# Expert slots dealt to the partitions in another order, and row gathers and stores over 128 partitions

## The chip, the core and the metric

The program runs on one core of one Trainium2 chip. A core has five engines that run their own instruction lists and meet only at semaphores: TensorE (PE, with its weight loads shown apart as PEld), VectorE (DVE), ScalarE (ACT), GpSimd (POOL) and SyncE (SP). Transfers are issued from SP's and from POOL's list and are carried by 16 DMA engines. The metric is the device time of one execution in microseconds (us), and the median of the runs is what counts.

## The reference

One decoder layer on 2048 tokens of width 1024, all in float32:

```python
h = rmsnorm(x, norm1_w)
x = x + mixer(h, w_in, ret_gn_w, conv_w, w_o)      # retention and short convolution
h = rmsnorm(x, norm2_w)
g_sel = top_1(softmax(h @ router_g_w + router_g_b))            # one group of 8
top_p, top_i = top_2(softmax(h @ router_e_w[g_sel] + ...))     # two of its 8 experts
y = segment_sum(gate * (silu(xb @ w_gate[e]) * (xb @ w_up[e])) @ w_down[e])
out = rmsnorm(x + y, final_norm_w)
```

There are 64 experts, each with 6 MB of weights (two matrices of 1024 by 512 and one of 512 by 1024). Each token goes to two experts, so the 64 experts receive 4096 rows in all, 64 on average.

## The kernel before

The first part (up to about 930 us in the profile) computes the mixer, adds the residual, writes the sums to the output in DRAM and the normalised rows to a DRAM tensor `h_rows`, and routes the tokens. Each token gets, for each of its two experts, a rank: how many earlier tokens chose that expert. `record` writes token number, a flag and the gate to a list in DRAM at slot `rank * 64 + expert` (indirect stores over 128 partitions, 128 indices each). Before the last 512 tokens are known, `load_list` reads the list of ranks 0 to 95 into the tile `listed`, rank r in partition r; the last 512 tokens are put in by TensorE (`place`), with a 0/1 matrix `here` that says which partition a rank belongs to. The sum is the tile `ix` of token numbers, one column for each expert, one partition for each of the 96 slots (`CAP`). A slot that holds no token has a number far above 2047.

The second part runs over 64 experts in a fixed order (`order`: one expert of each group in turn). The weights of an expert come as six transfers of 1024 KB ("units"), 128 partitions by 8 KB, issued from SP as soon as one of the buffers is free (14 buffers in the steady state, a little over two experts' worth). Most units are split by ACT (`split_hi`, L671) and DVE (`split_lo`, L677) into a rounded part and a remainder, and TensorE multiplies three products for each (L727 to L729); a quarter is multiplied whole (L1043).

The rows of an expert make three trips through POOL's queue, each one an indirect DMA with a column of `ix` as its indices: `gather` fetches normalised rows from `h_rows` (issued three experts ahead, L698), TensorE transposes them (`xpose`, L718), `regather` fetches the same tokens' residual rows from the output into the same tile (L705), the expert's result is added by DVE (`add_rows`), and `put_rows` stores them to the output (L811). Indices above 2047 are out of bounds and move nothing. A row is 4096 bytes. Seven row tiles are in use in turn. With these three trips an expert moves 3 x 4096 bytes for each of its rows.

On ACT, DVE and PE the order of work is the order in which the code is written. A transposed row tile is copied out of PSUM by ACT (L721) and DVE (L722), in the same two instruction lists that split the units.

Of the kernel before, what the change touches and what calls it, by code (L numbers as in the profile page):

```python
# [10 lines left out]
F32 = mybir.dt.float32  # L11
F32R = mybir.dt.float32r
BF16 = mybir.dt.bfloat16
I32 = mybir.dt.int32
U32 = mybir.dt.uint32
AF = mybir.ActivationFunctionType
OP = mybir.AluOpType
AX = mybir.AxisListType

P = 128  # L20
S = 2048
D = 1024
KD = D // P
# [4 lines left out]
NE = 64  # L28
# [3 lines left out]
CAP = 96  # L32
RANKS = CAP + S
NONE = 1 << 20
EPS = 1e-6
NROW = 7
# [8 lines left out]
Q, K, V, G, F0, F1, F2, O0, O1 = range(9)  # L45
CONV = {F0: "ccuu", F1: "ccuu", F2: "bbbb"}
CN = dict(ident=(0, 128), mhalf=(128, 132), tok=(148, 164), slots=(164, 260),
          mask=(260, 388), tri=(388, 516), vdec=(516, 520), odec=(520, 524), cdec=(524, 528))
NCON, NKEEP = 528, 260


def host_constants():
    f = np.float32
    c = np.zeros((P, NCON), f)
    i = np.arange(P)

    def put(name, a):
        lo, hi = CN[name]
        c[:, lo:hi] = a

    put("ident", np.eye(P))
    put("mask", i[:, None] <= i[None, :])
    put("tri", i[:, None] < i[None, :])
    log_g = np.log1p(-(2.0 ** (-5.0 - np.arange(H)))).astype(f).astype(np.float64)
    put("vdec", np.exp(-log_g[None] * (i[:, None] + 1)))
    put("odec", np.exp(log_g[None] * (i[:, None] + 1)) * P ** -0.5)
    put("cdec", np.exp(log_g * P)[None])
    put("tok", np.arange(S // P)[None] * P + i[:, None] - NONE)
    put("mhalf", -0.5)
    put("slots", np.arange(96)[None])  # L70
    inv = (10000.0 ** (-np.arange(64) / 64)).astype(f)
    ang = (np.arange(S).astype(f)[:, None] * inv[None]).astype(np.float64)
    cos, sin = np.cos(ang).T.astype(f), np.sin(ang).T.astype(f)
    rot = np.stack([np.concatenate([cos, cos]), np.concatenate([sin, -sin])], 1)
    empty = np.zeros((RANKS * NE, 4), f)
    return c, np.ascontiguousarray(rot), empty
# [3 lines left out]
def hybrid_layer(ctx: ExitStack, tc: tile.TileContext, x, xT, norm1, w_in, gn_w, conv_w, w_o, norm2, norm2r,  # L80
                 r_w, r_b, w_gate, w_up, w_down, final_w, con, rot, empty, out):
    nc = tc.nc
    act, dve, pool, pe, sp = nc.scalar, nc.vector, nc.gpsimd, nc.tensor, nc.sync

    h_d = nc.dram_tensor("h_rows", (S, D), F32, kind="Internal").ap()
    list_d = nc.dram_tensor("slots", (RANKS * NE, 4), F32, kind="Internal").ap()
# [6 lines left out]
    base = ctx.enter_context(tc.tile_pool(name="base", bufs=1, side="left"))  # L93
# [10 lines left out]
    def cst(name):  # L104
        lo, hi = CN[name]
        return cons[:, lo:hi] if hi <= NKEEP else cons2[:, lo - NKEEP:hi - NKEEP]

    ident, mask = cst("ident"), cst("mask")
# [84 lines left out]
    tri = late.tile([P, P], BF16, name="tri")  # L193
# [77 lines left out]
    rt = {}  # L271
# [228 lines left out]
    def small(shape, name, dt=F32, bufs=1, pool=late):  # L500
        return pool.tile([P] + shape, dt, name=name, bufs=bufs)

    def bc(ap, shape):
        return ap.to_broadcast([P] + shape)

    iota = cst("slots")
# [28 lines left out]
    def gates(b, i):  # L535
        c = rt["c", i]
        z, rec = c["z"], c["rec"]
        dve.reciprocal(z[:, 3:5], z[:, 3:5])
        dve.tensor_scalar(z[:, 0:3], z[:, 0:3], z[:, 3:4], None, op0=OP.mult)
        dve.reciprocal(z[:, 2:3], z[:, 2:3])  # L540
        dve.tensor_scalar(rec[:, :, 3], z[:, 0:2], z[:, 4:5], z[:, 2:3], op0=OP.mult, op1=OP.mult)
# [7 lines left out]
    def rank2(b, i):  # L549
        c = rt["c", i]  # L550
        prod = small([2, NE], "prod")
        rk, key = (small([2], n, bufs=2) for n in ("rk", "key"))
        dve.tensor_tensor(prod, c["full"], bc(c["p"][:, None, :NE], [2, NE]), op=OP.mult)
        dve.tensor_reduce(rk, prod, axis=AX.X, op=OP.add)
        if b == NB - 1:
            c["here"] = small([2, CAP], "here", bufs=2)
            dve.tensor_tensor(c["here"], bc(iota[:, None, :CAP], [2, CAP]), bc(rk[:, :, None], [2, CAP]), op=OP.is_equal)
        dve.scalar_tensor_tensor(key, rk, float(CAP), c["e64"], op0=OP.is_ge, op1=OP.add)
        for j in range(2):
            dve.tensor_tensor(c["rec"][:, j, 2:3], key[:, j:j + 1], key[:, 1 - j:2 - j], op=OP.is_gt)  # L560
        c["rk"], c["slot"] = rk, small([2], "slot", I32, bufs=8, pool=base)
# [18 lines left out]

    def load_list():
        t = late.tile([CAP, NE, 4], F32, name="listed")
        sp.dma_start(t, list_d[:CAP * NE].rearrange("(s e) r -> s e r", e=NE))
        pool.tensor_scalar(t[:, :, 0], t[:, :, 0], float(NONE), None, op0=OP.add)
        rt["listed"] = t

# [31 lines left out]
    EX = {}  # L618
# [55 lines left out]
    def split_lo(i):  # L674
        if i < len(pieces):
            hi, lo, src = parts[pieces[i]]
            dve.tensor_tensor(lo, src, hi.bitcast(F32), op=OP.subtract)  # L677
# [3 lines left out]
    def moved(kind, q, ins):  # L681
        for (k2, q2), o in rows_dma.items():
            if order[q2] // 8 != order[q] // 8:
                tc.declare_no_dep(ins.ins, o.ins, reason="tokens of another group")
        rows_dma[kind, q] = ins

    def row_of(q):
        return EX["rows"][q % NROW]

    def spaced(t=spacer):  # L690
        pool.memset(t, 0.0)

    def gather(q):
        if q >= NE:
            return
        e = order[q]
        spaced()
        pool.indirect_dma_start(out=row_of(q), out_offset=None, in_=h_d,  # L698
                                in_offset=bass.IndirectOffsetOnAxis(ap=EX["ix"][:, e:e + 1], axis=0),
                                bounds_check=S - 1, oob_is_err=False)  # L700

    def regather(q):
        e = order[q]
        spaced()
        i = pool.indirect_dma_start(out=row_of(q), out_offset=None, in_=out,  # L705
                                    in_offset=bass.IndirectOffsetOnAxis(ap=EX["ix"][:, e:e + 1], axis=0),
                                    bounds_check=S - 1, oob_is_err=False)
        moved("g", q, i)
# [100 lines left out]
    def put_rows(q):  # L809
        spaced()  # L810
        i = pool.indirect_dma_start(out=out, out_offset=bass.IndirectOffsetOnAxis(ap=EX["ix"][:, order[q]:order[q] + 1], axis=0),  # L811
                                    in_=row_of(q), in_offset=None, bounds_check=S - 1, oob_is_err=False)
        moved("s", q, i)


# [11 lines left out]
    for b in range(NB):  # L827
# [12 lines left out]
        for g in (F0, F1):  # L840
            for j in range(2):
                f = j + 2 * (g == F1)
# [16 lines left out]
        if b < NB - 1:  # L859
# [5 lines left out]
            for i in range(TB):  # L865
# [7 lines left out]
                at(so + 2 * i + 7, address, b, i)  # L873
                at(so + 2 * i + 7, record, b, i)
    at(start[NB - 1, F1], load_list)

    for k in range(KD):
# [24 lines left out]
    b = NB - 1  # L902
# [46 lines left out]
    i = TB - 1  # L949
# [9 lines left out]
    rank1(b, i)  # L959
    spread(i, dve, 0)  # L960
    rank2(b, i)
    place(i, 0)
    gates(b, i - 1)
    ix = base.tile([CAP, NE], I32, name="ix")
    li, sec, nsec = (base.tile([CAP, NE], F32, name=n) for n in ("li", "sec", "nsec"))
    EX.update(li=li, ix=ix, sec=sec, nsec=nsec)
    listed = rt["listed"]
    dve.tensor_tensor(ix, listed[:, :, 0], rt["pslot", 0][:CAP, :NE], op=OP.add)
    split_lo(0)
    split_lo(1)  # L970
    spread(i - 1, dve, 2)
# [9 lines left out]

    w = ctx.enter_context(tc.tile_pool(name="work", bufs=1, side="right", reuse_waits="tile"))
    EX["work"] = w
    EX["rows"] = [w.tile([CAP, D], F32, name=f"row{i}") for i in range(3)]

    def clear(q):
        act.activation(row_of(q).rearrange("p (a b) -> p a b", b=P),
                       ident[:CAP, None, :].to_broadcast([CAP, KD, P]), AF.Copy, scale=0.0)

    def pair(tag):  # L990
        t = raw.tile([P, 2, D], F32, name="pair", tag=tag)
        return [t[:CAP, i] for i in range(2)]

    for q in range(3):
        clear(q)
# [2 lines left out]
    for q in range(3):  # L998
        gather(q)
    split_lo(2)  # L1000
    xpose(0)
    regather(0)
    for k in range(3, LEAD):
        split_lo(k)
# [9 lines left out]
    for i, (q, wi, c) in enumerate(estream):  # L1014
# [7 lines left out]
        if i in (36, 40, 44):  # L1022
            two = pair(FIRST[i // 4 - 9])
            if i < 44:
                EX["rows"] += two
                for j in (2, 1):
                    clear(len(EX["rows"]) - j)
                    if i == 36:
                        gather(5 - j)
            else:  # L1030
                EX["fw"], EX["fwm"] = two
                sp.dma_start(EX["fw"], bass.AP(tensor=final_w.tensor, offset=final_w.offset, ap=[[0, CAP], [1, D]]))
        n = q, 2 * wi + c // 4
        cs = slice(c % 4 * 512, c % 4 * 512 + 512)
# [12 lines left out]
        if wi < 2:  # L1047
# [3 lines left out]
            if wi == 0 and c == 0:  # L1051
                if q > 1:
                    gather(q + 3)
                if later(q - 2):
                    weights(q - 2)
            if wi == 0 and c == 2 and 1 < q < NG + 2:
                put_rows(q - 2)
# [12 lines left out]
        else:  # L1070
# [15 lines left out]
            else:  # L1086
                if c == 1:
                    norm1_rows(q - 1)
                if c == 2:
                    r = row_of(q - 1)  # L1090
# [114 lines left out]
```

## Time and profile before

| | |
|---|---|
| runs | 2198.74, 2205.43, 2206.37 us, median 2205.43 |
| profiled execution | 2198.08 us, of which the span of instructions is 2196.3 us |
| granted TensorE clock, mean | 0.988 of full speed |
| PE busy | 2127.2 us, 97% of the span |
| DVE, ACT, POOL busy | 73%, 56%, 40% |
| moved by DMA | 578.70 MB, mean 263 GB/s |
| of that from SP's queue and from POOL's queue | 526.43 MB and 50.44 MB |

"Share" of DMA is the mean busy share of the 16 DMA engines; it can come out a little over 1, since a packet's time is taken from its start to its end and neighbours overlap slightly. A matmul's busy time overlaps the next one's, so PE at 97% says less than the pace at which experts follow one another, for which the issue of each expert's `regather` is a good mark: it stands once in each expert, behind the transposition of that expert's rows.

### The profile page before, as it was taken

How to read it: one execution, taken by the hardware profiler on the slowest of the kernel's cores; microseconds unless marked ns; L12 is line 12 of the kernel's file. 1: busy time of each engine (PE TensorE's matmuls, PEld its weight loads, DVE VectorE, ACT ScalarE, POOL GpSimd, SP SyncE). 2: the span in 40 equal slices, each digit the busy share in tenths (PEclk: the TensorE clock that was granted, in tenths of full speed). 3: DMA queues.
4: the chain of work that ended last, by engine and by line, in shares of the span. 5: the costliest groups of instructions: out<-in, count | busy, mean ns of one | idle time of the engine just before them, and what ended most of it. 6: DMA issues, size and time to landing. Idle time of an engine off the chain costs nothing. (4 is left out here: it accounts for less than half of the span.)

```text
span 2196.3 us, 28309 instructions
## 1 busy us (share of the span) xinstructions
PE 2127.2 (97%) x9673; PEld 1562.2 (71%) x9674; DVE 1612.1 (73%) x2393; ACT 1226.1 (56%) x1881; POOL 871.1 (40%) x927
## 2 busy tenths in 40 slices
PE   8999999999999999789999999999999999999997
PEld 7888888888888888666666666666666665666664
DVE  5667566656666666678888888878888787788886
ACT  5324342433343323566667777767676666667674
POOL 0020031002200120341247777666555655565657
PEclk9999999999999999899999999999999999999999
DMA  8335344524443456689999999999999999999994
GB/s 269 117 99 179 96 144 130 168 87 154 128 160 96 135 156 237 231 285 352 365 368 369 367 360 353 356 355 362 357 359 350 356 352 353 355 355 352 358 356 158
DMA packets 136100, 578.70 MB, mean 263 GB/s; under 512 B 23440, under 2 KB 23792, under 8 KB 86736
## 3 DMA queue, kind: packets, MB, share of 16 engines
q1 hardware_dynamic: 113424, 526.43, 67.9%
q0 software_dynamic: 22528, 50.44, 7.1%
q8 instruction: 76, 1.25, 0.2%
q14 instruction: 72, 0.59, 0.1%
HBM read 559.94 MB, written 44.20 MB: 275 GB/s over the span
## 5 line engine op out<-in xcount | busy, mean ns | idle before, releaser
L677 DVE TENSOR_TENSOR ring<-unit,ring 128x1024 fp32r<-128x1024 f32 x428 | 557.9, 1325 | 124.4 <-ACT ring L671 122.7
L671 ACT ACTIVATE ring<-unit 128x1024 fp32r<-128x1024 f32 x428 | 444.4, 1054 | 232.5 <-DMA unit<-in_w_gate_dram 105.5
L291 PE MATMUL acc<-hhi,ring 128*128 128x512 f32 x1280 | 403.8, 393 | 6.9 <-ACT ring L166 5.8
L677 DVE TENSOR_TENSOR part<-unit,part 128x1024 fp32r<-128x1024 f32 x212 | 275.8, 1314 | 57.7 <-ACT part L671 57.0
L167 DVE TENSOR_TENSOR ring<-wraw,ring 128x512 fp32r<-128x512 f32 x256 | 172.7, 687 | 185.1 <-ACT ring L166 184.9
L166 ACT ACTIVATE ring<-wraw 128x512 fp32r<-128x512 f32 x256 | 154.0, 626 | 263.9 <-issue 111.0
L727 PE MATMUL acc<-ring,xhi 128*96 128x512 f32 x684 | 288.4, 422 | 4.4 <-ACT xhi L721 4.0
L729 PE MATMUL acc<-ring,xlo 128*96 128x512 f32 x684 | 272.9, 399 | 16.0 <-DVE xlo L722 16.0
L671 ACT ACTIVATE part<-unit 128x1024 fp32r<-128x1024 f32 x212 | 221.0, 1054 | 115.7 <-DMA unit<-in_w_gate_dram 42.9
L291 PEld LDWEIGHTS acc<-hhi,ring 128*128 128x128 f32 x1280 | 241.0, 188 | 56.3 <-ACT ring L166 5.5
L728 PE MATMUL acc<-ring,xhi 128*96 128x512 f32 x684 | 272.5, 398 | 0.0
L291 PE MATMUL acc<-hlo,ring 128*128 128x512 f32 x640 | 249.9, 390 | 0.0
L1043 PE MATMUL acc<-unit,ewhole 128*96 128x512 f32 x512 | 230.3, 592 | 0.0
L291 PE MATMUL acc<-ring,mix 128*128 128x512 f32 x768 | 185.4, 396 | 0.0
L729 PEld LDWEIGHTS acc<-ring,xlo 128*96 128x96 f32 x684 | 111.9, 164 | 71.9 <-DVE xlo L722 24.2
L291 PEld LDWEIGHTS acc<-ring,mix 128*128 128x128 f32 x768 | 142.7, 189 | 28.5
L291 PE MATMUL acc<-ring,hhi 128*128 128x512 f32 x512 | 162.3, 398 | 0.0
L1043 PEld LDWEIGHTS acc<-unit,ewhole 128*96 128x96 f32 x512 | 83.5, 163 | 110.6 <-issue 101.5
L727 PEld LDWEIGHTS acc<-ring,xhi 128*96 128x96 f32 x684 | 113.6, 166 | 63.4 <-ACT xhi L721 14.5
L728 PEld LDWEIGHTS acc<-ring,xhi 128*96 128x96 f32 x684 | 112.3, 164 | 50.3 <-issue 6.6
L727 PE MATMUL acc<-part,xhi 128*96 128x512 f32 x340 | 143.4, 422 | 4.7 <-ACT xhi L721 4.7
L783 POOL TENSOR_TENSOR pair<-pair 96x1024 f32<-96x1024 f32 x31 | 84.5, 2726 | 152.2 <-ACT pair L780 152.1
(229 smaller groups left out, 3732.5 us busy)
## 6 DMA issues: line engine op xcount, KB each, us to landing
unit<-in_w_down_dram SPq DMA_DIRECT2D x128, 1024.0 KB, 25.2
unit<-in_w_gate_dram SPq DMA_DIRECT2D x128, 1024.0 KB, 25.5
unit<-in_w_up_dram SPq DMA_DIRECT2D x128, 1024.0 KB, 26.8
wraw<-in_w_in_dram SPq DMA_DIRECT2D x225, 256.0 KB, 2.9
wraw<-in_w_o_dram SPq DMA_DIRECT2D x64, 256.0 KB, 2.9
xs<-in_x_dram SPq DMA_DIRECT2D x16, 512.0 KB, 4.8
x<-in_x_dram SPq DMA_DIRECT2D x16, 512.0 KB, 4.0
out_dram<-x SPq DMA_DIRECT2D x16, 512.0 KB, 4.0
```

Of the source, the lines that this page charges most:

```text
L166: act.activation(hi, src, AF.Copy)
L167: dve.tensor_tensor(lo, src, hi.bitcast(F32), op=OP.subtract)
L291: pe.matmul(o, l, r, start=first and j == 0, stop=last and j == 2)
L671: act.activation(t[:, 0], src, AF.Copy)
L677: dve.tensor_tensor(lo, src, hi.bitcast(F32), op=OP.subtract)
L727: pe.matmul(o, ahi, whi, start=first, stop=False)
L728: pe.matmul(o, ahi, wlo, start=False, stop=False)
L729: pe.matmul(o, alo, whi, start=False, stop=last)
L783: pool.tensor_tensor(r, r, m, op=OP.mult)
L1043: pe.matmul(o, whole[:, k - hi.shape[1]], wt, start=False, stop=last)
```

## The change

The ranks are dealt to the partitions in another order, by the table `RUNS`: partitions 0 to 31 hold ranks 0 to 31, partitions 32 to 63 hold ranks 64 to 95, partitions 64 to 95 hold ranks 32 to 63. The list is loaded by three transfers of 32 partitions instead of one of 96, and `here` compares with a row of constants `ranks` (96 columns more in the constants) instead of the plain count 0 to 95. The tile of indices grows to 128 partitions; the upper 32 are set out of bounds by one DVE instruction. The row tiles are 128 partitions high, and gathers, regathers and stores name all 128 partitions; the arithmetic still works on the first 96.

```diff
+RUNS = (0, 64, 32)
+    put("ranks", np.concatenate([np.arange(r, r + 32) for r in RUNS])[None])
...
-            dve.tensor_tensor(c["here"], bc(iota[:, None, :CAP], [2, CAP]), bc(rk[:, :, None], [2, CAP]), op=OP.is_equal)
+            dve.tensor_tensor(c["here"], bc(cst("ranks")[:, None], [2, CAP]), bc(rk[:, :, None], [2, CAP]), op=OP.is_equal)
...
     def load_list():
         t = late.tile([CAP, NE, 4], F32, name="listed")
-        sp.dma_start(t, list_d[:CAP * NE].rearrange("(s e) r -> s e r", e=NE))
+        lists = list_d[:CAP * NE].rearrange("(s e) r -> s e r", e=NE)
+        for i, r in enumerate(RUNS):
+            sp.dma_start(t[32 * i:32 * i + 32], lists[r:r + 32])
...
+    def row_all(q):
+        return EX["rows"][q % NROW]
+
     def row_of(q):
-        return EX["rows"][q % NROW]
+        return row_all(q)[:CAP]
...
-        pool.indirect_dma_start(out=row_of(q), out_offset=None, in_=h_d,
+        pool.indirect_dma_start(out=row_all(q), out_offset=None, in_=h_d,
                                 in_offset=bass.IndirectOffsetOnAxis(ap=EX["ix"][:, e:e + 1], axis=0),
...
-        i = pool.indirect_dma_start(out=row_of(q), out_offset=None, in_=out,
+        i = pool.indirect_dma_start(out=row_all(q), out_offset=None, in_=out,
...
         i = pool.indirect_dma_start(out=out, out_offset=bass.IndirectOffsetOnAxis(ap=EX["ix"][:, order[q]:order[q] + 1], axis=0),
-                                    in_=row_of(q), in_offset=None, bounds_check=S - 1, oob_is_err=False)
+                                    in_=row_all(q), in_offset=None, bounds_check=S - 1, oob_is_err=False)
...
-    ix = base.tile([CAP, NE], I32, name="ix")
+    ix = base.tile([P, NE], I32, name="ix")
+    dve.tensor_scalar(ix[CAP:], iota[CAP:, :NE], float(NONE), None, op0=OP.add)
...
-    dve.tensor_tensor(ix, listed[:, :, 0], rt["pslot", 0][:CAP, :NE], op=OP.add)
+    dve.tensor_tensor(ix[:CAP], listed[:, :, 0], rt["pslot", 0][:CAP, :NE], op=OP.add)
...
-    EX["rows"] = [w.tile([CAP, D], F32, name=f"row{i}") for i in range(3)]
+    EX["rows"] = [w.tile([P, D], F32, name=f"row{i}") for i in range(3)]
```

The order of instructions stays as it was on every engine, but for one instruction on DVE and two transfers on SP. On POOL, in the middle of the expert stage, one expert's share of the list reads before (`pair` and `row` are row tiles, `sec`, `nsec` and `oss` columns of per-slot factors):

```order
401 L705 DMA pair<-out_dram,ix 96x1024
402 L783 TENSOR_TENSOR row_7826<-row_7826,pair 96x1024
403 L691 MEMSET spacer 1x1
404 L811 DMA out_dram<-row_7826,ix 2048x1024
405 L691 MEMSET spacer 1x1
406 L698 DMA row_7825<-h_rows,ix 96x1024
```

and now:

```order
401 L715 DMA pair<-out_dram,ix 128x1024
402 L793 TENSOR_TENSOR row_7829<-row_7829,pair 96x1024
403 L701 MEMSET spacer 1x1
404 L821 DMA out_dram<-row_7829,ix 2048x1024
405 L701 MEMSET spacer 1x1
406 L708 DMA row_7828<-h_rows,ix 128x1024
```

The same transfers stand in the same places, with 128 destinations where there were 96; the store shows the shape of the output, and its source has grown in the same way.

On DVE, at the passage from the first part to the expert stage, where `ix` is made (`rec`, `zexp` belong to the routing of the last tokens), stood before:

```order
1080 L541 TENSOR_SCALAR rec<-zexp 128x2
1081 L968 TENSOR_TENSOR ix<-listed,acc 96x64
1082 L677 TENSOR_TENSOR ring<-unit,ring 128x1024 x2
```

and stands now:

```order
1080 L545 TENSOR_SCALAR rec<-zexp 128x2
1081 L975 TENSOR_SCALAR ix<-cons 32x64
1082 L979 TENSOR_TENSOR ix<-listed,acc 96x64
1083 L683 TENSOR_TENSOR ring<-unit,ring 128x1024 x2
```

One instruction on 32 partitions has come in ahead of the one that the first gather waits for.

## Rows read from the trace of the kernel before

**Rows 1.** Page, parts 1 and 3: busy time; DMA queues.
```profile
PE 2127.2 (97%) x9673; PEld 1562.2 (71%) x9674; DVE 1612.1 (73%) x2393; ACT 1226.1 (56%) x1881; POOL 871.1 (40%) x927
...
q1 hardware_dynamic: 113424, 526.43, 67.9%
q0 software_dynamic: 22528, 50.44, 7.1%
```

**Rows 2.** POOL's timeline, three regathers: start us, length us, instruction, idle before.
```profile
1005.95 0.97 POOL L705 DMA_INDIRECT pair<-out_dram,ix  x1 [9.90 <-PE pxg L718]
...
1397.68 1.08 POOL L705 DMA_INDIRECT pair<-out_dram,ix  x1 [2.68 <-PE pxg L718]
...
2152.95 2.10 POOL L705 DMA_INDIRECT row<-out_dram,ix  x1 [0.43 <-issue]
```

**Rows 3.** Groups by line, regathers from 1397 to 2153.1 us: busy, mean ns.
```profile
L705 POOL DMA_INDIRECT pair<-out_dram,ix x23 | 27.6, 1201 | 11.0 <-PE pxg L718 5.5 <-issue 4.9 <-PE acc L729 0.6
L705 POOL DMA_INDIRECT row<-out_dram,ix x16 | 23.1, 1446 | 10.3 <-PE pxg L718 5.7 <-issue 4.5
```

**Rows 4.** Waits from 1397.6 to 2153 us: total us, times, longest us.
```profile
ACT ring L671 <- DMA unit<-in_w_gate_dram: 100.6, 45, 3.8
...
ACT part L671 <- DMA unit<-in_w_gate_dram: 42.9, 19, 3.0
ACT ring L671 <- DMA unit<-in_w_up_dram: 33.6, 31, 1.7
...
PE acc L729 <- DVE xlo L722: 20.9, 20, 1.2
ACT part L671 <- DMA unit<-in_w_up_dram: 15.0, 14, 1.8
PE acc L727 <- ACT xhi L721: 8.6, 10, 1.8
```

**Rows 5.** Stretches of the expert stage: last three columns clock, DMA share, GB/s.
```profile
1000.00:1006.00 6.00, 6.00 (x32) 4.47 (x31) 5.25 (x6) 4.62 (x6) 0.05 (x1) 1.00 1.02 426
1006.00:1012.00 6.00, 6.00 (x21) 3.11 (x20) 4.43 (x7) 3.21 (x4) 2.05 (x4) 1.00 0.95 362
1012.00:1018.00 6.00, 6.00 (x30) 4.36 (x29) 5.07 (x5) 3.70 (x5) 1.75 (x2) 1.00 0.95 345
1018.00:1024.00 6.00, 6.00 (x31) 4.41 (x30) 5.12 (x6) 4.62 (x8) 0.00 (x0) 1.00 1.02 425
...
1100.00:1400.00 300.00, 300.00 (x1288) 199.13 (x1287) 243.67 (x255) 219.04 (x284) 206.49 (x169) 1.00 0.99 362
1400.00:2150.00 750.00, 720.22 (x3017) 468.12 (x3016) 615.66 (x606) 516.05 (x680) 445.75 (x409) 0.99 1.00 356
```

**Rows 6.** Indirect transfers by tile: issue time on POOL in ns, least, median, most.
```profile
L573 POOL DMA_INDIRECT slots<-rec,slot x32: 954/958/1998, 301.7 to 956.2; - x32
...
L698 POOL DMA_INDIRECT row<-h_rows,ix x28: 956/1964/2760, 930.6 to 2110.3; - x28
```

**Rows 7.** Timelines of DVE, POOL and PE where the expert stage begins.
```profile
929.48 0.26 DVE L968 TENSOR_TENSOR ix<-listed,acc 96x64 int32<-96x64 f32 x1
...
930.58 2.76 POOL L698 DMA_INDIRECT row<-h_rows,ix  x1 [5.00 <-DVE ix L968]
...
939.57 1.20 PE L718 MATMUL pxg<-cons,row 96*128 96x96 f32 x6 [4.58 <-DMA row<-h_rows,ix]
```

**Rows 8.** Page, part 6: transfers by line, KB each, median us to landing.
```profile
unit<-in_w_gate_dram SPq DMA_DIRECT2D x128, 1024.0 KB, 25.5
...
pair<-h_rows,ix POOLq DMA_INDIRECT x36, 10.4
...
cons<-in_con_dram SPq DMA_DIRECT2D x1, 134.0 KB, 4.1
...
listed<-slots SPq DMA_DIRECT2D x1, 96.0 KB, 2.4
```

More of the change, by code (lines that the diff above doesn't have):

```diff
@@ L47 @@
 CN = dict(ident=(0, 128), mhalf=(128, 132), tok=(148, 164), slots=(164, 260),
-          mask=(260, 388), tri=(388, 516), vdec=(516, 520), odec=(520, 524), cdec=(524, 528))
-NCON, NKEEP = 528, 260
+          mask=(260, 388), tri=(388, 516), vdec=(516, 520), odec=(520, 524), cdec=(524, 528), ranks=(528, 624))
+NCON, NKEEP = 624, 260
+RUNS = (0, 64, 32)
 def host_constants():
@@ L983, in hybrid_layer @@
     EX["work"] = w
-    EX["rows"] = [w.tile([CAP, D], F32, name=f"row{i}") for i in range(3)]
+    EX["rows"] = [w.tile([P, D], F32, name=f"row{i}") for i in range(3)]
     def clear(q):
-        act.activation(row_of(q).rearrange("p (a b) -> p a b", b=P),
-                       ident[:CAP, None, :].to_broadcast([CAP, KD, P]), AF.Copy, scale=0.0)
+        act.activation(row_all(q).rearrange("p (a b) -> p a b", b=P),
+                       ident[:, None, :].to_broadcast([P, KD, P]), AF.Copy, scale=0.0)
     def pair(tag):
         t = raw.tile([P, 2, D], F32, name="pair", tag=tag)
-        return [t[:CAP, i] for i in range(2)]
+        return [t[:, i] for i in range(2)]
     for q in range(3):
@@ L1030, in hybrid_layer @@
             else:
-                EX["fw"], EX["fwm"] = two
+                EX["fw"], EX["fwm"] = (t[:CAP] for t in two)
                 sp.dma_start(EX["fw"], bass.AP(tensor=final_w.tensor, offset=final_w.offset, ap=[[0, CAP], [1, D]]))
```

## The prediction

> **What bounds the kernel now.** Busy shares come first, and they mislead: PE is busy 97% of the span [rows 1], so it looks like the one bound. The second view is the pace of the experts. From the regather at 1005.95 to that at 1397.68 lie 21 experts (one regather in each), so one takes (1397.68 - 1005.95) / 21 = 18.65 us [rows 2]. From 1397.68 to 2152.95 there are 23 + 16 = 39 regathers [rows 3], so 38 experts take 755.27 us, 19.88 us each. PE's work is the same for every expert; something else sets the pace in the second stretch, and costs 38 x (19.88 - 18.65) = 46.5 us.
>
> The waits of that stretch say what: ACT, in `split_hi`, waits for unit transfers 100.6 + 42.9 + 33.6 + 15.0 = 192 us, while PE itself shows 30 us of waiting, for the row splits that stand behind the late weight splits on ACT and DVE [rows 4]. So the transfers are late and the wait is handed down. Before 1397 the units fetched ahead covered it: 25 experts pass at PE's pace before the first long interval.
>
> Third, the DMA engines by stretches. In six microseconds with unit transfers alone they move 425 to 426 GB/s at a share of 1.02; in the neighbouring stretches, where a regather and a gather, then a store, are under way, only 362 and 345 GB/s, at 0.95 [rows 5]. One expert needs six units of 1024 KB, 6.29 MB, and on average 3 x 64 x 4096 bytes = 0.79 MB of rows, 7.08 MB in all. In 18.65 us that is 380 GB/s; from 1400 to 2150 the engines give 356 at a share of 1.00 [rows 5]. The bound is the transfers, and what lowers their rate is the rows.
>
> **The change part by part.** (1) *Which engine carries which row.* No row of the trace names the engine of a packet, so this part rests on an assumption: that 96 indices go to the 16 engines in runs of six, and 128 indices by blocks of four partitions, so that partitions 0 to 63 go round engines 0 to 7 and partitions 64 to 127 round engines 8 to 15. The Trainium skill, "DMA: Bandwidth & Descriptors", section "The descriptor swizzle", gives just this map for a transfer to 128 partitions; no run here shows it, and it says nothing of indirect ones. Under the assumption an expert of 64 rows gives six rows to each of 10.7 engines and none to the others before, and four rows to each of 16 engines after.
>
> The price. POOL's queue has 7.1% of 16 engines' span [rows 1]: 0.071 x 16 x 2196.3 = 2495 us of one engine, 39.0 per expert. On 10.7 engines that is 3.65 us each, on 16 engines 2.44. Six units at 425.5 GB/s take 14.78 us. So the fullest engines own 14.78 + 3.65 = 18.43 us of work per expert before; the pace is 19.88, so 1.45 us come from rows and units hindering each other (the fall from 425 to 345 with shares near 0.95 is both, idle engines and slower packets). After: 14.78 + 2.44 = 17.22 us on the mean engine. The experts are not equal, though. From the reference, 29 of 64 have more than 64 tokens (36 to 85); summed over all experts the fullest six engines carry 384 rows of a trip each before, the mean being 256, while after one engine carries 363, the next 318 and 291. The fullest one has 363/384 of 3.65 = 3.45.
>
> What the hindering becomes is the unknown. If it shrinks with the rows on an engine (six to four), it is 0.97, and the fullest engine's pace is 14.78 + 3.45 + 0.97 = 19.20; if it stays, 19.68; if it vanishes, 18.23, under PE's 18.65. The cover counts too: before, the deficit of 19.88 - 18.65 = 1.23 us was hidden for 25 experts, some 31 us. The loss is then 64 x (pace - 18.65) - 31: nothing for 18.23, 4 us for 19.20, 35 us for 19.68, against 46.5 now. The gain lies between 11.5 and 46.5 us; I take 38 (a loss of 8.5), near the middle case, because only one engine remains that full.
>
> (2) *32 more indices in each of 192 indirect DMAs.* On POOL an indirect DMA over 128 partitions takes 954 ns at least, one over 96 takes 956 [rows 6]: issuing costs nothing more. The queue's 22528 packets [rows 1] are 192 x (96 + 16) + 32 x 32, so an index out of bounds counts as a packet too, and each engine gets 3 x 32 / 16 = 6 more per expert. At the mean of the queue's packets, 2495 us / 22528 = 0.11 us, that is 0.66 us per expert; but the 3 x 4096 rows of 4096 bytes make 50.33 of its 50.44 MB, so the empty ones carry nothing and must be far below the mean. Between 0 and 0.66 us; I take 0. At the upper end the fullest engine's pace is 19.86, and nothing is gained.
>
> (3) *The passage to the experts.* PE waits 4.58 us for the first gather [rows 7], which stands in a queue of three with the last units. Four rows instead of six per engine can shorten it by between 0 and 4.58; I take 1.0, since the landing also has a part that rows do not set (10.4 us from issue to landing in the stage, 2.4 us for a small plain load) [rows 8]. The added DVE instruction is a third the height of the one behind it, of 0.26 us [rows 7], and delays POOL by at most that: +0.2. The three loads of the list in place of one stand in SP's list long before `ix` needs them, in the last block of the first part, and cost nothing.
>
> (4) *Constants.* 96 columns more, 48 KB beside loads of 134 and 130 KB that land in 4.1 us [rows 8], in the first microseconds when the loads for the first product are due: 0 to 1.5 us; I take 0.3. The clears, transpositions and sums keep their length, since they work on partitions side by side.
>
> Sum, on the profiled execution's 2198.08 us: -38 - 1.0 + 0.2 + 0.3 = 2159.6, forecast 2160. That execution is 7 us below the median 2205.43 of the runs and at the lower end of their spread; a kernel that goes at PE's pace to the end should scatter less, so I add nothing.
>
> **The rivals.**
>
> *The transfers are bound by their sum, not by the fullest engine.* Then dealing rows differently changes nothing and the pace stays 19.88: 2198 to 2206. An empty packet at the mean's price ends here too. For it: the share is 1.00 from 1400 to 2150 [rows 5], as if no engine had room. Against: a share counts a packet as busy while it waits, and 425 GB/s without rows shows that the sum has no lid at 356. The Trainium skill ("DMA: Bandwidth & Descriptors", "Specifications") has such a lid, 358 GB/s from HBM for each core; the 425 GB/s of this core, alone on the chip, go past it, so the trace does not agree. By that rule the change would be worth nothing, which is this rival. A lid may still lie in mixing random rows with streams. Chance 0.18.
>
> *Consecutive runs stay: eight partitions to an engine.* Then the holes in the new order hurt: partitions 0 to 31 and 64 to 95 are eight engines with eight rows each, the others have next to none. The fullest engine's rows take 3.65 x 8/6 = 4.87 us. With the hindering of today the pace is 14.78 + 4.87 + 1.45 = 21.10, the loss 64 x 2.45 - 31 = 126 instead of 46.5: 2278 us; without any, 19.65, the loss 33 and 2185. The middle is 2231. It decides for slower from 0.2 us of hindering on. For it: the runs of six assumed for 96, of which it is the plain continuation; 128 indices are not gathered anywhere in this trace. Against: only the skill's map. Chance 0.17.
>
> *All of the wait goes.* 18.65 us for every expert: 2198.08 - 46.5 - 0.5 = 2151. For it: the share of 0.95 beside 345 GB/s, if the slower packets too come from rows crossing to other engines' partitions. Against: the engine with 363 rows. It belongs to the forecast's own range.
>
> **How the numbers follow.** The forecast with its bounds (2147 to 2188, 2147 being the full gain plus the 4.58 us of the first wait) has 0.65; no change 0.18; runs of eight 0.17. The predicted time is 2160. For 8 in 10 the range must take in the no-change case: 2147 to 2214, which leaves the slower rival out. About 0.5%, 11 us, can be told from no change against 2205.43. Faster: 0.64 of the forecast and 0.03 of the runs of eight, 0.67; the same: 0.01 + 0.15 + 0.01 = 0.17; slower: the rest of the two rivals, 0.16.
>
> **What would show it.** Right: regathers 18.7 to 19.2 us apart up to the last, ACT's waits for units under 80 us, a rate over 365 GB/s from 1400 on, and over 345 with a share near 1 in the stretches with rows. No relief in the hindering would show as long intervals that begin later than the 25th expert. Wrong by the sum: intervals of 19.9 as before. Wrong by runs of eight: the first long intervals near the 12th expert (31 / 2.45), and a share below 0.95 in stretches with rows. A first PE wait longer than 4.58 us would show that gathers of 128 indices themselves land later.

## The result and the profile after

The changed kernel takes 2152.69 us (median of 4 runs, 2152.0 to 2153.47) against 2202.09 us before (4 runs on the same chip, 2198.43 to 2206.37): a ratio of 0.9775, 95% interval 0.9752 to 0.9798. The forecast was 2160 us. The profiled execution's span is 2151.0 us, 45.3 us less than the 2196.3 us of the profiled execution before.

Parts 1 and 3 of the page after, busy time and DMA queues, against [rows 1]:

```profile
PE 2113.4 (98%) x9673; PEld 1561.2 (73%) x9674; DVE 1573.0 (73%) x2394; ACT 1235.7 (57%) x1881; POOL 960.9 (45%) x927
...
q1 hardware_dynamic: 113456, 526.48, 65.1%
q0 software_dynamic: 28672, 50.46, 6.2%
```

The same bytes go through both queues. POOL's queue has 28672 - 22528 = 6144 = 192 x 32 packets more, the empty ones, and yet its packets take a smaller share.

The regathers of the changed kernel from 1290 us on, as groups: count, duration in ns (least, median, most), first and last start in us.

```profile
L715 POOL DMA_INDIRECT pair<-out_dram,ix x25: 1085/1094/1111, 1307.5 to 2090.9; - x25
L715 POOL DMA_INDIRECT row<-out_dram,ix x19: 1085/1096/1109, 1326.1 to 2109.6; - x19
```

That is 44 regathers, 43 intervals in 2109.6 - 1307.5 us: 18.65 us each, PE's pace, up to the last. Before, the 38 intervals from 1397.68 on took 19.88 [rows 2, 3]. No stretch of long intervals is left. The last regather comes 2152.95 - 2109.6 = 43.4 us earlier than in [rows 2].

Waits from 1397.6 to 2110 us in the changed kernel: total, times, longest.

```profile
ACT ring L677 <- PE acc L739: 103.1, 102, 3.2
...
ACT part L677 <- PE acc L739: 48.4, 50, 3.2
...
ACT ring L677 <- DMA unit<-in_w_up_dram: 0.7, 2, 0.3
```

In [rows 4] ACT waited 192 us for units; now 0.7 us, and for the rest it waits for PE to free its buffers. PE's own waits for row splits are gone from the list.

Stretches of the changed kernel (columns as in [rows 5]: PE, PEld, DVE, ACT, POOL, clock, DMA share, GB/s):

```profile
1006.00:1012.00 6.00, 6.00 (x31) 4.29 (x30) 5.83 (x8) 4.58 (x7) 2.78 (x3) 1.00 1.01 426
1012.00:1018.00 6.00, 6.00 (x21) 3.24 (x20) 3.78 (x5) 1.91 (x3) 2.27 (x4) 1.00 0.84 313
1018.00:1024.00 6.00, 6.00 (x29) 4.36 (x28) 4.95 (x6) 5.03 (x8) 0.00 (x0) 1.00 1.01 399
...
1400.00:2100.00 700.00, 700.00 (x3000) 463.21 (x2999) 572.42 (x602) 521.18 (x674) 529.30 (x410) 1.00 0.95 379
```

PE is busy throughout, and the transfers give 379 GB/s, just what 7.08 MB in 18.65 us need, at a share of 0.95: the engines now have time to spare. The low 313 GB/s stands beside a share of only 0.84: here units are not slow but wait for a free buffer, as SP's queue shows for 1012 to 1018 us (total, times, longest):

```profile
SPq L637 <- PE acc L1054: 9.4, 1, 9.4
```

The kernel before has the same wait of 9.4 us from 1002 to 1012 us, so a part of the low 362 and 345 GB/s in [rows 5] may be units not yet issued, too. The lightened kernels below separate the two.

The passage to the experts, POOL's and then PE's timeline of the changed kernel (start, length, instruction, idle before):

```profile
934.87 2.83 POOL L708 DMA_INDIRECT row<-h_rows,ix  x1 [5.38 <-ACT row L998]
```

```profile
941.99 1.52 PE L728 MATMUL pxg<-cons,row 96*128 96x96 f32 x8 [2.65 <-DMA row<-h_rows,ix]
```

PE's first wait for rows is 2.65 us instead of 4.58 [rows 7]. The first gather itself was issued 4.3 us later than in [rows 7]; in the other kernels below, whose first part is nearly the same, it stands anywhere from 930.7 to 933.8 us, so most of that is scatter of the first part. PE's first wait scatters too: 2.65 to 4.35 us in the profiles of the kernels with a new order or 128 destinations, 4.58 and 5.50 us in the two that have neither.

Landings after, from part 6 of the page and the view of DMA issues:

```profile
unit<-in_w_gate_dram SPq DMA_DIRECT2D x128, 1024.0 KB, 5.8
...
pair<-h_rows,ix POOLq DMA_INDIRECT x36, 10.6
...
cons<-in_con_dram SPq DMA_DIRECT2D x1, 182.0 KB, 4.2
...
listed<-slots SPq DMA_DIRECT2D x3, 32.0 KB, 1.9
```

A `w_gate` unit lands 5.8 us after its issue instead of 25.5, a gather as late as before (10.6 and 10.4) [rows 8].

### The profile page after: what moved, and what is told of

Read it like the earlier page. It is cut to its first block, busy times and chain, and to the rows that moved or that the text cites. A ratio compares the mean times of both kernels' runs of the same rounds, so it can differ in the third digit from the quotient of the medians.

```text
span 2151.0 us, 28313 instructions
## 1 busy us (share of the span) xinstructions
PE 2113.4 (98%) x9673; PEld 1561.2 (73%) x9674; DVE 1573.0 (73%) x2394; ACT 1235.7 (57%) x1881; POOL 960.9 (45%) x927
## 3 DMA queue, kind: packets, MB, share of 16 engines
q0 software_dynamic: 28672, 50.46, 6.2%
## 5 line engine op out<-in xcount | busy, mean ns | idle before, releaser
L683 DVE TENSOR_TENSOR ring<-unit,ring 128x1024 fp32r<-128x1024 f32 x428 | 524.5, 1243 | 73.3 <-ACT ring L677 70.8
L683 DVE TENSOR_TENSOR part<-unit,part 128x1024 fp32r<-128x1024 f32 x212 | 260.7, 1238 | 36.4 <-ACT part L677 35.3
L784 POOL TENSOR_SCALAR oss<-oss,sec,nsec 96x1 f32<-96x1 f32 x55 | 164.8, 2997 | 5.9
L737 PEld LDWEIGHTS acc<-ring,xhi 128*96 128x96 f32 x684 | 112.7, 165 | 53.9 <-issue 10.6
```

What stands on the lines that cost most here:

```text
L737: pe.matmul(o, ahi, whi, start=first, stop=False)
L784: pool.tensor_scalar(ss, ss, EX["sec"][:, e:e + 1], EX["nsec"][:, e:e + 1], op0=OP.mult, op1=OP.add)
```

## The experiments: which part of the change does it

The change has two parts that can be taken apart: the order of the ranks, and the 128 destinations, and the latter for each of the three trips. Two theories: the *fullest engine* alone sets the pace (rows per engine), or *crossing* does, rows carried by an engine whose own block of partitions they do not belong to (if the prediction's maps hold, with 96 indices in runs of six all rows but a few cross, and with 128 indices none). From the reference's routing (36 to 85 tokens in an expert) the fullest engine's rows of one trip, summed over the 64 experts, are under those maps 384 before, 363 after, 512 for the plain order over 128, and 313 for an order made even for runs of six. Divided by 64 this is 6.00, 5.67, 8.00 and 4.89 rows in a trip.

**The order alone.** All three trips over 96 partitions, the new table kept:

```diff
-        pool.indirect_dma_start(out=row_all(q), ... ap=EX["ix"][:, e:e + 1] ...
+        pool.indirect_dma_start(out=row_of(q), ... ap=EX["ix"][:CAP, e:e + 1] ...
```

and so for `regather` and `put_rows`. Expected:

> The new order of the ranks (0-31, 64-95, 32-63), but gathers, regathers and stores over 96 partitions as before. Theory A, the fullest engine decides: with runs of six partitions to an engine the full engines still carry 18 rows per expert on some ten engines, so the time stays that of before, 2198 to 2206 us, experts 19.9 us apart from about the 25th on. Theory B, what decides is that an engine's rows go to partitions which other engines fill with units (packets slow each other): the crossing stays but is spread over both halves of the partitions, so a part of the gain, 2165 to 2195 us.

Measured: 2182.11 us (2179.93 to 2182.45), ratio 0.991, 0.9892 to 0.9927. Its regathers from 1290 us on:

```profile
L715 POOL DMA_INDIRECT pair<-out_dram,ix x25: 1084/1084/1881, 1304.6 to 2117.5; - x25
L715 POOL DMA_INDIRECT row<-out_dram,ix x19: 1073/1084/2067, 1323.2 to 2139.2; - x19
```

43 intervals in 834.6 us, 19.41 on the mean: the long intervals are back. And its stretches:

```profile
1100.00:1400.00 300.00, 300.00 (x1289) 198.82 (x1288) 245.26 (x259) 221.52 (x287) 209.16 (x169) 1.00 0.99 373
...
1400.00:2100.00 700.00, 680.44 (x2877) 445.02 (x2876) 573.71 (x572) 491.07 (x645) 447.34 (x396) 0.99 1.00 359
```

A share of 1.00 at 359 GB/s, as before the change. Under runs of six the new order is no more even than the old one (384 rows both), so by theory A it should have gained nothing; it gains 20 of the 49 us, with 373 GB/s from 1100 to 1400 where [rows 5] had 362. Theory B had foretold such a part, since the rows now go to both halves of the partitions. The lightened kernels below don't bear that out, so the reason stays open.

**The 128 partitions alone.** The table gives the plain order:

```diff
-RUNS = (0, 64, 32)
+RUNS = (0, 32, 64)
```

> The changed kernel with the ranks in plain order (0-31, 32-63, 64-95), gathers and stores over 128 partitions. If 128 indices are dealt by blocks of four partitions, eight engines carry eight rows of a trip each and the others nearly none. Theory A, the fullest engine decides: rows take 3.65 x 8/6 = 4.87 us on it, more than in the kernel before, so slower than before, 2210 us or more. Theory B, crossing decides: no engine writes another's partitions, packets keep their length, 14.78 + 24 x 0.157 = 18.5 us per expert (0.157 us is 4096 bytes at 425.5/16 GB/s), below PE's 18.65, so 2152 to 2165 us.

Measured: 2151.88 us (2150.46 to 2153.59), ratio 0.9772, 0.9754 to 0.9789. Its expert stage:

```profile
1400.00:2100.00 700.00, 700.00 (x2998) 463.07 (x2997) 572.58 (x601) 521.14 (x674) 529.78 (x410) 1.00 0.97 377
```

PE never stops: the whole gain, at the lower edge of theory B's range, although under the map the fullest engine now carries eight rows of a trip, more than the six before the change. The fullest engine alone is not the bound; this theory falls in its pure form.

**Even rows over 96.** An order in which each run of six partitions has four ranks below 64 and two of the last 32; all trips over 96:

```diff
+DEAL = [4 * (p // 6) + p % 6 if p % 6 < 4 else 64 + 2 * (p // 6) + p % 6 - 4 for p in range(96)]
-    put("ranks", np.concatenate([np.arange(r, r + 32) for r in RUNS])[None])
+    put("ranks", np.array(DEAL)[None])
-        for i, r in enumerate(RUNS):
-            sp.dma_start(t[32 * i:32 * i + 32], lists[r:r + 32])
+        for k in range(6):
+            sp.dma_start(t[k::6], lists[k:64:4] if k < 4 else lists[60 + k::2])
```

> 96 partitions in all transfers, the ranks dealt so that each run of six partitions holds four ranks below 64 and two of 64 to 95: every engine carries four rows of an expert with 64, but its rows go to partitions that other engines fill. The list is loaded by six transfers of every sixth partition. Theory A, the fullest engine decides: the whole gain, 2152 to 2162 us. Theory B, crossing decides: little of it, 2180 to 2206 us.

Measured: 2149.94 us (2149.72 to 2152.66), ratio 0.9767, 0.975 to 0.9785.

```profile
1400.00:2100.00 700.00, 700.00 (x3000) 463.44 (x2999) 572.52 (x599) 521.15 (x677) 527.87 (x411) 1.00 1.01 378
```

Again the whole gain, 2 us under theory A's range, now with all three trips crossing: crossing alone is not the bound either, and theory B (2180 us or more) falls in its pure form too. But the share is 1.01 where the plain order over 128 has 0.97 and the change 0.95, so these engines have nothing to spare. In all three PE's pace hides how far the transfers are from it.

**Stores alone over 96, gathers alone over 96.** The edit of the first run in `put_rows` only:

```diff
-                                    in_=row_all(q), in_offset=None, bounds_check=S - 1, oob_is_err=False)
+                                    in_=row_of(q), in_offset=None, bounds_check=S - 1, oob_is_err=False)
```

> The changed kernel with the stores alone over 96 partitions (order of ranks and gathers as changed). Theory A: the fullest engines carry 4 + 4 + 6 rows per expert, 14 instead of 12, under PE's pace, 2152 to 2160 us. Theory B: a third of the row trips crosses, 2152 to 2180 us, and the stretches with a store show a DMA rate as low as before (345 GB/s or less), those with gathers do not.

and its mirror, the edit in `gather` and `regather` only:

```diff
-        pool.indirect_dma_start(out=row_all(q), ... ap=EX["ix"][:, e:e + 1] ...
-        i = pool.indirect_dma_start(out=row_all(q), ... ap=EX["ix"][:, e:e + 1] ...
+        pool.indirect_dma_start(out=row_of(q), ... ap=EX["ix"][:CAP, e:e + 1] ...
+        i = pool.indirect_dma_start(out=row_of(q), ... ap=EX["ix"][:CAP, e:e + 1] ...
```

> The changed kernel with gathers and regathers over 96 partitions and only the stores over 128 (the mirror of the run with stores alone over 96, which took 2150.6 us). The rank order is the new one, so gathers and regathers put rows on engines in runs of six that write into other engines' partitions. If the crossing counts in the gathers' and regathers' writes: two of three trips cross, the transfers' pace is between that of order only (about 19.5 us per expert) and that of the change; with two thirds of the distance 18.9 to 19.1, which the 31 us of cover hide nearly whole: 2150 to 2160 us, with long intervals only near the end. If crossing in the gathers is all that counts: like order only, 2176 to 2188 us. If it is the stores that count: 2150 to 2154, all intervals 18.7.

Stores over 96: 2150.6 us (2148.42 to 2152.18), ratio 0.9768, 0.9751 to 0.9786; its stage:

```profile
1400.00:2100.00 700.00, 700.00 (x3001) 463.57 (x3000) 572.67 (x599) 521.24 (x676) 531.44 (x412) 1.00 0.95 378
```

Gathers over 96: 2184.51 us (2180.34 to 2187.07), ratio 0.9919, 0.989 to 0.9947; its stage:

```profile
1400.00:2100.00 700.00, 679.84 (x2872) 444.15 (x2871) 573.04 (x571) 490.27 (x644) 436.83 (x395) 0.99 1.00 359
```

The one is the change, within 1 GB/s; the other is the order alone, as it was expected for the case that the gathers are all that counts. What the 128 destinations bring lies in the two gathers, which write rows into the tiles. The stores, which read them, may stay at 96.

## The transfers' own pace, with PE's work made lighter

PE's 18.65 us hide every pace below it. In six more kernels the third product of each split multiplication of the experts is left out, so that PE has less to do and the transfers show their own pace:

```diff
         pe.matmul(o, ahi, whi, start=first, stop=False)
-        pe.matmul(o, ahi, wlo, start=False, stop=False)
-        pe.matmul(o, alo, whi, start=False, stop=last)
+        pe.matmul(o, ahi, wlo, start=False, stop=last)
```

> The kernel before with the third product of the split multiplications in the expert stage left out (remainder of the activations times rounded weights), so that PE needs about 14 us per expert instead of 18.65 and the transfers set the pace alone. This and the next three runs read the transfers' own pace for each dealing. Both theories: 19.3 to 19.9 us between regathers, as in its slow stretch.

> The changed kernel with the same product left out. Theory A, the fullest engine decides and nothing else changed: 14.78 + 3.45 + 1.45 = 19.7 us per expert. Theory B, the packets also keep their length because no engine writes another's partitions: 14.78 + 17 x 0.157 = 17.4 us. DVE, busy 572 of 700 us at 18.65 us per expert, needs 15.3 us per expert and would be no bound.

> Ranks in plain order over 128 partitions (512 rows of a trip on the fullest engine over all experts, mean 256), the same product left out. Fullness alone: 14.78 + 4.87 + 1.45 = 21 us per expert, slower than the kernel before. Packets at full length only: 14.78 + 24 x 0.157 = 18.5 us; between this and the changed kernel's lies the price of unequal engines without crossing.

> Even runs of six over 96 partitions (313 rows on the fullest engine), the same product left out. Without crossing it would be 14.78 + 14.7 x 0.157 = 17.1 us per expert; with packets as slow as in the kernel before (a share of 1.01 was seen at 18.65 us), 18.2 to 18.6 us. The distance to the changed kernel is the price of crossing alone.

> Light run: the kernel with gathers and regathers over 96 partitions and stores over 128, with the third product of each split multiplication of the experts left out, so that the transfers set the pace. Pace of the changed kernel's light run 17.78 us per expert, of even rows with crossing (other order of the ranks, all trips over 96) 19.12. If every trip that crosses costs the same: 17.78 + 2/3 x (19.5 - 17.78) = 18.9. If the gathers' writes alone count: about 19.5. If the stores alone count: 17.8.

> Light run: the kernel with stores over 96 partitions and gathers and regathers over 128, with the third product of each split multiplication of the experts left out, so that the transfers set the pace. If every trip that crosses costs the same: 17.78 + 1/3 x (19.5 - 17.78) = 18.35 us per expert. If only writes into the partitions count: 17.8. If only the stores' reads count: about 19.5.

The kernel before, with PE's work lightened, takes 2206.42 us, ratio to the kernel before 1.0018, 1.0006 to 1.0029: a third of the split products gone, and nothing gained. That settles the first point of the prediction. The changed kernel, lightened, takes 2076.97 us, ratio 0.9432, 0.9404 to 0.9459. Six-microsecond stretches of the kernel before, lightened, and its long one:

```profile
1000.00:1006.00 6.00, 6.00 (x30) 4.32 (x29) 5.86 (x6) 5.95 (x9) 1.75 (x2) 1.00 1.00 355
1006.00:1012.00 6.00, 6.00 (x27) 3.69 (x26) 6.00 (x8) 5.29 (x7) 2.27 (x4) 1.00 1.00 421
1012.00:1018.00 6.00, 6.00 (x27) 4.03 (x26) 6.00 (x8) 3.93 (x7) 3.08 (x1) 1.00 1.04 329
...
1290.00:1990.00 700.00, 573.35 (x2100) 333.56 (x2100) 572.06 (x560) 476.35 (x629) 402.67 (x385) 0.93 1.00 355
```

And of the changed kernel, lightened:

```profile
1006.00:1012.00 6.00, 6.00 (x25) 3.62 (x24) 6.00 (x8) 3.23 (x5) 2.10 (x1) 1.00 1.00 416
1012.00:1018.00 6.00, 6.00 (x33) 4.53 (x32) 6.00 (x7) 6.00 (x11) 6.00 (x1) 1.00 1.02 416
1018.00:1024.00 6.00, 6.00 (x20) 3.08 (x19) 6.00 (x9) 3.23 (x4) 5.77 (x3) 1.00 1.01 419
...
1290.00:1990.00 700.00, 612.54 (x2379) 363.86 (x2377) 648.06 (x634) 539.27 (x713) 529.59 (x435) 0.96 1.01 400
```

The dips to 329 and 355 are gone: with rows under way the engines move 416 to 419 GB/s, little below units alone. Over 700 us it is 400 against 355. DVE is at 648 of 700 us here, so the pace of this run is only an upper bound for the transfers'; the same holds for the lightened kernel with stores over 96, where DVE is at 652.

The regathers from 1290 us on of the lightened kernels, the kernel before first:

```profile
L705 POOL DMA_INDIRECT pair<-out_dram,ix x25: 1073/1084/1085, 1307.2 to 2143.8; - x25
L705 POOL DMA_INDIRECT row<-out_dram,ix x19: 1084/1084/2032, 1324.2 to 2163.4; - x19
```

the changed kernel:

```profile
L715 POOL DMA_INDIRECT pair<-out_dram,ix x24: 1085/1096/1860, 1337.9 to 2010.7; - x24
L715 POOL DMA_INDIRECT row<-out_dram,ix x18: 1085/1096/1927, 1302.9 to 2031.9; - x18
```

the plain order over 128:

```profile
L715 POOL DMA_INDIRECT pair<-out_dram,ix x24: 1085/1671/2121, 1359.8 to 2075.1; - x24
L715 POOL DMA_INDIRECT row<-out_dram,ix x19: 1086/1694/4026, 1300.8 to 2098.0; - x19
```

even rows over 96:

```profile
L716 POOL DMA_INDIRECT pair<-out_dram,ix x24: 1073/1084/2112, 1366.5 to 2091.5; - x24
L716 POOL DMA_INDIRECT row<-out_dram,ix x19: 1073/1084/2034, 1310.2 to 2113.3; - x19
```

gathers over 96:

```profile
L715 POOL DMA_INDIRECT pair<-out_dram,ix x25: 1062/1073/2102, 1299.4 to 2136.0; - x25
L715 POOL DMA_INDIRECT row<-out_dram,ix x19: 1062/1073/1963, 1320.3 to 2156.0; - x19
```

and stores over 96:

```profile
L715 POOL DMA_INDIRECT pair<-out_dram,ix x24: 1097/1107/1870, 1341.0 to 2012.5; - x24
L715 POOL DMA_INDIRECT row<-out_dram,ix x19: 1102/1107/1943, 1292.5 to 2031.7; - x19
```

From the first start to the last, by the intervals between, each gives a pace per expert; beside it what two prices make of it (below):

| lightened kernel | time, us | pace, us | by two prices |
|---|---|---|---|
| before: plain order, 96 | 2206.42 | 856.2 / 43 = 19.91 | taken |
| gathers over 96, new order | 2202.13 | 856.6 / 43 = 19.92 | 19.85 |
| even rows over 96 | 2155.89 | 803.1 / 42 = 19.12 | 18.97 |
| plain order over 128 | 2144.41 | 797.2 / 42 = 18.98 | taken |
| the change | 2076.97 | 729.0 / 41 = 17.78 | 17.76 |
| stores over 96, new order | 2077.1 | 739.2 / 42 = 17.60 | 17.81 |

One engine's units take 14.78 us by the prediction. All that lies above is here put on the rows of the fullest engine, as an estimate. Plain order over 128 has 3 x 8 rows on it: (18.98 - 14.78) / 24 = 0.175 us a row. Before the change there are 6 stored rows and 12 gathered over 96: (19.91 - 14.78 - 6 x 0.175) / 12 = 0.34 us for a gathered one. With 0.175 for every row stored, or gathered over 128, and 0.34 for every row gathered over 96, the other four come out within 0.21 us. So both theories are needed: the fullest engine's rows count, and a row gathered over 96 weighs on the pace like two. The expectations, which priced the two apart, missed some of these paces: 18.98 lies between their cases (18.5 and 21), as does 17.78 (17.4 and 19.7); 19.12 lies above both of its cases (at most 18.6), and 19.92 above all of its own (at most 19.5).

The price isn't the time of the row's own packet. The traces hold every packet's size and time; this is what they give for the lightened kernels from 1290 to 1990 us:

| lightened kernel | unit packets of 8192 bytes: mean, median, share over 400 ns | row packets of 4096 bytes, all three trips: mean, median |
|---|---|---|
| before | 365 ns, 314 ns, 23% | 192 ns, 181 ns |
| gathers over 96, new order | 364 ns, 316 ns, 27% | 190 ns, 185 ns |
| even rows over 96 | 349 ns, 314 ns, 18% | 193 ns, 178 ns |
| plain order over 128 | 347 ns, 309 ns, 6% | 161 ns, 159 ns |
| the change | 326 ns, 309 ns, 3% | 163 ns, 159 ns |
| stores over 96, new order | 325 ns, 309 ns, 3% | 162 ns, 159 ns |

While gathers go over 96, about a fifth of the unit packets take over 400 ns; while they go over 128, few do, whatever the order of the ranks. On the mean an engine carries 768 / 16 = 48 unit packets and 192 / 16 = 12 row packets of an expert. 365 against 326 ns is then 1.9 us per expert, and 192 against 163 ns is 0.35 us: together about the 2.13 us between 19.91 and 17.78, and most of it in the units. A packet's time may hold waiting as well, so the mean of the plain order over 128, raised by a few very long packets, can't be split further.

With lightened PE the order alone, in the guise of gathers over 96, gains nothing (19.92 against 19.91), as the count of 384 rows says. That it gains 20 us beside the full work of PE is not explained by these prices; there, from 1100 to 1400 us, 373 GB/s flow instead of 362, and from 1400 on 359, little above the 356 of before.

## A version faster than both

If the transfers have 18.65 - 17.78 = 0.87 us an expert to spare, work can be moved off PE. A whole multiplication of a chunk takes PE 0.43 us and spares ACT and DVE a split; half of these are made split ones:

```diff
-        return w == 2 and c >= 4
+        return w == 2 and c >= 6
-    NH = 2
+    NH = 3
```

> The changed kernel with half of its whole multiplications (L663, c >= 6 in place of c >= 4, and NH 3 in place of 2) turned into split ones. PE's work per expert falls: four chunks that took 4 x 0.43 us whole become two whole and two in three products of 0.23 us each, 0.33 us less; ACT gets 1.05 us and DVE 1.33 us more per expert (DVE about 16.6 of 18.3 us). After the change the transfers' own pace (17.78 us in the run with a third of the split products left out) lies under PE's, so PE's pace sets the time: 64 x 0.33 = 21 us less than the change, 2131 us, all intervals near 18.3. Rival: DVE or ACT, now at nine tenths, fall behind in stretches and PE waits for the splits: 2145 to 2170 us, with PE's waits naming DVE ring or part.

Measured: 2130.86 us (2130.42 to 2131.61), ratio to the kernel before 0.9675, 0.9652 to 0.9699. Its regathers from 1290 us on, and its stage:

```profile
L715 POOL DMA_INDIRECT pair<-out_dram,ix x25: 1085/1094/1544, 1297.8 to 2064.8; - x25
L715 POOL DMA_INDIRECT row<-out_dram,ix x19: 1085/1096/1109, 1316.0 to 2083.1; - x19
```

```profile
1400.00:2050.00 650.00, 650.00 (x2925) 451.28 (x2923) 610.15 (x607) 533.34 (x678) 445.60 (x392) 1.00 0.98 389
```

785.3 / 43 = 18.26 us an expert, PE without a pause, DVE at 610 of 650 us and the transfers at 0.98: three resources are now near their ends together. The time is the expected one. Shortening PE's work shortened the changed kernel by the expected amount, so PE bounds it.

## Why the prediction was right, step by step

The forecast was near, but the time says little about the steps: the four kernels with PE's full work whose lightened pace is at most 19.12 us all come out at 2150 to 2153 us, because PE and the cover hide the rest. That it came so near with two terms too dear is in part luck.

- *The bound*: right. Lightening PE by a third of its split products leaves the kernel before where it was.
- *Evening out the rows*, the reason given for the gain: a part of it. The 128 destinations in plain order bring the whole gain with eight rows on the fullest engine in place of six, a kernel that the prediction's prices would make slower than before (4.87 + 1.45 us above the units). Evening them out takes another 18.98 - 17.78 = 1.2 us off the pace, which PE hides.
- *The map of rows to engines*: not seen, since no record names the engine of a packet. The Trainium skill's map ("DMA: Bandwidth & Descriptors", "The descriptor swizzle"), stated for a plain transfer, agrees with the runs: by runs of eight partitions both orders over 128 would put eight rows on the fullest engine, while the paces are 17.78 and 18.98.
- *"The fullest one has 363/384 of 3.65 = 3.45"*: too dear. The pace leaves at most 17.78 - 14.78 = 3.00 for rows and hindering together. The 3.65 came from the queue's share, in which the gathered rows of the kernel before count with their longer packets. The changed kernel's row packets, 0.163 us each when lightened, make 17 x 0.163 = 2.77 us on the fullest engine.
- *"If it shrinks with the rows on an engine (six to four), it is 0.97"*: the step that was mis-sized. Units and rows do hinder each other (unit packets of 365 ns against 326), but not in proportion to the rows on an engine: it hangs on the gathers' 96 destinations and goes nearly whole with the 128. What is left of it is at most 3.00 - 2.77 = 0.23 us. Undoing the 128 in the gathers alone brings 19.92 back, undoing them in the stores changes nothing. So the pace fell under PE's, the loss was 0 and not 8.5 us, and the time came out 7 us below the forecast, where the prediction's last case (2151) had it.
- *Cover of 31 us*: it holds where it was not meant. Paces of 18.98 and 19.12 lose 64 x 0.33 = 21 and 64 x 0.47 = 30 us, just within it. That fits the plain order over 128 and the even rows over 96 each taking as little time as the change.
- *Empty indices at 0*: right. The queue has 6144 packets of 4 bytes more than before, and its packets of 4 bytes take 9 ns (median) in the trace of the changed kernel; six more on each engine are 0.05 us per expert, not 0.66.
- *The passage*: PE's first wait fell by 1.9 us where 1.0 was taken; the constants land 0.1 us later (4.2 against 4.1). Both are below the scatter of the first part.
- *The rivals*: bound by the sum, no change: refuted by 400 GB/s with rows, against 355. The Trainium skill's limit of 358 GB/s ("DMA: Bandwidth & Descriptors", "Specifications"), half of what it gives for a memory stack with two cores, does not bind this core alone on its chip. Runs of eight: the 2185 to 2278 us that it gave did not come, and the two orders over 128 differ in pace (above).
- *Its marks*: the intervals, ACT's waits and the rate from 1400 on were as foretold; "over 345 with a share near 1 in the stretches with rows" was not (313 at 0.84), since units wait for buffers there. The mark would have needed a kernel that is still bound by transfers; in the lightened one it holds (416 at 1.02).

What stays open: why gathers over 96 lengthen the units' packets. That rows cross to another engine's partitions fits. The Trainium skill ("SBUF — State Buffer", "Door 1: The DMA port swizzle") gives each group of eight partitions (two blocks of four) one port of its own; if so, rows and units of different engines would meet at it. But no run gathers over 128 with crossing, or over 96 without, so the runs show the price and not the port. Where the rows land doesn't settle the pace by itself: in such groups of eight, plain order puts eight rows of a trip on the fullest group over 96 (19.91 us) as over 128 (18.98), and the new order 5.67 over 96 (19.92) as over 128 (17.78).

## What to carry to other kernels

Give an indirect gather into on-chip memory all 128 partitions, even where it fills fewer (the rest out of bounds), and measure; stores didn't ask for it here. Deal the filled partitions over both halves as well (here ranks 32 to 63 in partitions 64 to 95): over 128 partitions that took 1.2 us off an expert's 18.98 where nothing hid it. When a change hides one bound behind another, make the hiding engine's work lighter in a trial: three kernels with equal times had paces of 17.78, 18.98 and 19.12 us beneath. What comes free on the bound removed can be spent on the one that took its place.

## What was not expected of the hardware

- In the lightened kernels with gathers over 96 partitions 18 to 27% of the unit packets take over 400 ns, in those with gathers over 128 partitions 3 to 6% (median 309 to 316 ns in all). Stores make no such difference.
- A gathered 4 KB row weighs on the pace as 0.34 us over 96 partitions and as 0.175 us over 128, an estimate from two paces that fits four others within 0.21 us; the row packets themselves take 0.19 and 0.16 us on the mean.
- Indices out of bounds count as packets of 4 bytes (6144 more in the queue) and take 9 ns each.
